# GpSimd takes the first product of three norms and the gated MLP's product, ScalarE the scale and shift

## The chip, the cores and the metric

The kernel runs on one core of a Trainium2 chip. The metric is the device time of one execution in microseconds (us). The kernel before took 2484.61 us, the median of three runs (2483.22 to 2488.88). Five engines work side by side, each in the order of its own queue: TensorE (PE; PEld for its weight loads), VectorE (DVE), ScalarE (ACT), GpSimd (POOL) and SyncE (SP), which issues the large transfers.

## What is computed

A decoder trunk of two layers on 256 tokens of width 2048, all in float32. Every sub-layer is

```python
h = modulate(rms_norm(x, norm_g), shift, scale)   # x / rms * g * (1 + scale) + shift
x = x + gate * sublayer(h)
```

The sub-layers are, in order: a gated MLP (`z = gelu(h @ w_in + b_in)`, `u, v = split(z)`, v goes through a layer norm and a causal mixing over 128 tokens, then `(u * v) @ w_out`), a squared-ReLU MLP, attention with three branches (its keys and values come from a norm of their own, its queries from another), and a second squared-ReLU MLP. A last RMSNorm ends it.

## The kernel before

**Layout.** x lies in SBUF transposed, as 16 tiles `x[:, k, :]` of 128 features by 256 tokens. Every activation that goes into a product is kept as a pair of float32r tiles, `hi` (the rounded value) and `lo` (the rest). Every weight block is split in the same way into `wh` and `wl`, so that each product is three matmuls: wh by hi, wl by hi, wh by lo (L221 to L223).

**The stream.** One queue of 1 MB blocks comes from HBM through the tile `raw`. A weight block is two halves of two k each: ScalarE rounds a half to `wh` (L194), VectorE makes `wl` (L195). Between them lie blocks of the modulation matrices, each one VectorE instruction with an accumulator (L184). `get` keeps up to three halves ready ahead of TensorE. One half feeds 24 matmuls of 256 columns: two k by four output tiles by three.

**The norms.** Where a norm comes ahead of a product there are two ways. In three of the sub-layers (both squared-ReLU MLPs and the key and value projection) the first slab of 512 outputs runs on x scaled without 1/rms (`gemm_first`, L426), and `settle` multiplies 1/rms in afterwards. While that slab runs, from its half 4 on, the normed tiles for the other slabs are made, one closure for each k in `self.todo` (L456), which `norm_until` calls: up to k 5 within the first slab, the other ten in the second slab (`gemm_b`, L226, two k ahead of what TensorE takes). A step of `normed` is three instructions: VectorE multiplies x, 1/rms and the gain (L330), ScalarE adds the shift and rounds to `hi` (L333), VectorE makes `lo` (L334). The intermediate `ht` shares three buffers (tag `t2k`) with the tiles of `settle`, of the rotary embedding and of the MLP. The norm at the start and that of the queries call `normed` directly and are not touched.

**The gated MLP.** In the U half, `mix` (L748) takes a pair of output tiles out of PSUM: two gelu on ScalarE, `u` times the mixed v on VectorE (L755), rounding on ScalarE (L382), low parts on VectorE (L383). There are 16 pairs, in two groups of four slabs, between which the first half of the output product runs. `split` (L380) is the helper that rounds and makes the low parts; it has many other callers.

**Order.** A scheduler arranges the instructions of each engine when the program is built, by program order as priority and its own estimate of when operands are ready; on the chip each queue then runs strictly in that order. So an instruction that waits holds up everything behind it on its engine.

Of the kernel before, what the change touches and what calls it, by code (L numbers as in the profile page):

```python
# [9 lines left out]
F32 = mybir.dt.float32  # L10
F32R = mybir.dt.float32r
AF = mybir.ActivationFunctionType
# [5 lines left out]
T = 256  # L18
KT = D // 128
# [19 lines left out]
def run(gen):  # L39
    for _ in gen:  # L40
        pass
# [21 lines left out]
class Kernel:  # L63
# [259 lines left out]
    def normed(self, rb, g, s, hs, ks=range(KT)):  # L323

        nc = self.nc
        for k in ks:
# [10 lines left out]
            self.last_norm = (hi, lo)  # L337
            hs.append(both)

    def modulation(self, name, g, k0=0, k1=KT):  # L340

        nc = self.nc
        m, b, gs = self.modr[name], self.modb[name], self.modg[name]
        assert all((name, o + k) in self.made for o in (0, KT) for k in range(k0, k1)), name
        for o in (0, KT):
            nc.vector.tensor_add(out=m[:, o + k0:o + k1], in0=m[:, o + k0:o + k1], in1=b[:, o + k0:o + k1])
        nc.vector.scalar_tensor_tensor(
            out=gs[:, k0:k1], in0=m[:, KT + k0:KT + k1], scalar=1.0, in1=g[:, k0:k1], op0=ALU.add, op1=ALU.mult
        )
        return gs, m[:, 0:KT]  # L350
# [26 lines left out]
            for f in range(n * 4 + pair * 2, n * 4 + pair * 2 + 2):  # L377
                nc.scalar.mul(self.x[:, f, :], self.x[:, f, :], self.g_final[:, f:f + 1])

    def split(self, src, hi, lo):  # L380
        nc = self.nc
        nc.scalar.copy(out=hi, in_=src)  # L382
        nc.vector.tensor_sub(out=lo, in0=src, in1=hi.bitcast(F32))  # L383

    def shifted(self, pool, n):

# [39 lines left out]
    def gemm_first(self, hs, evac, spare=False):  # L426

        nc = self.nc  # L430
        if spare:
            row = [self.acc.tile([128, 512], F32, name="acc") for _ in range(2)]
        ps = [self.acc.tile([128, 512], F32, name="acc") for _ in range(4)]
        gs, s, _ = self.coming
        keep = self.keep = self.tmp.tile([128, T], F32, name="rbs", bufs=1)

        def mm(wh, wl, f, k, kk):
            fs = slice(f * 128, (f + 1) * 128)
            (hi, lo), o = self.xs[kk], ps[f]
            nc.tensor.matmul(o[:, 0:T + 2], wh[:, k, fs], hi, start=kk == 0, stop=False, skip_group_check=True)  # L440
            nc.tensor.matmul(o[:, 0:T + 2], wl[:, k, fs], hi, start=False, stop=False, skip_group_check=True)  # L441
            nc.tensor.matmul(o[:, 0:T], wh[:, k, fs], lo, start=False, stop=kk == KT - 1, skip_group_check=True)  # L442

        for half in range(8):
            wh, wl = self.get()
            if half < 7:
                for k in range(2):
                    for f in range(4):
                        mm(wh, wl, f, k, 2 * half + k)
                if half == 3:  # L450
                    if not spare:
                        row = [self.aux.tile([128, 512], F32, name="aux") for _ in range(2)]
                    sd = self.rms_column(row[0])
                elif half == 4:
                    nc.scalar.copy(out=keep, in_=self.rms_row(sd, row[1]))
                    self.todo = iter([lambda k=k: self.normed(keep, gs, s, hs, (k,)) for k in range(KT)])  # L456
                    self.n_normed = 0
                if half >= 4:
                    self.norm_until(2 * half - 6)
            else:  # L460
                for pair in range(2):
                    for f in range(2 * pair, 2 * pair + 2):
                        for k in range(2):
                            mm(wh, wl, f, k, 2 * half + k)
                    evac(pair, ps[2 * pair:2 * pair + 2])
# [153 lines left out]
    def gmlp(self, vec, vp, bv, vctx):  # L619
        tc, nc, A = self.tc, self.nc, self.A  # L620
        b_u, ln_g, ln_b, b_out = vec["b_u"], vec["ln_g"], vec["ln_b"], vec["b_out"]
        with ExitStack() as ctx:
# [7 lines left out]
            hs = []  # L630
# [32 lines left out]
            for at, (slabs, kq) in enumerate(V_ORDER):  # L663
# [5 lines left out]
                keep = at + 1 < len(V_ORDER) and V_ORDER[at + 1][0] is slabs  # L669
# [23 lines left out]
            def layer_norm():  # L693
                for tb in range(2):
                    nc.vector.bn_aggr(out=mv[:, tb, :], in_=stats[:, tb, :, :])
                nc.scalar.activation(out=rs, in_=mv[:, :, 1], func=AF.Sqrt, bias=self.eps)
                nc.vector.reciprocal(out=rs, in_=rs)
                nc.vector.scalar_tensor_tensor(
                    out=mv[:, :, 0], in0=mv[:, :, 0], scalar=-1.0, in1=rs, op0=ALU.mult, op1=ALU.mult
                )  # L700

            def normalise(n):
                for tb in range(2):
                    o = v[:, tb, n * 512:(n + 1) * 512]
                    nc.scalar.activation(
                        out=o, in_=o, func=AF.Identity, scale=rs[:, tb:tb + 1], bias=mv[:, tb, 0:1]
                    )

            def mixed(g):


                w = vs.tile([128, 128], F32, name="ws")
                nc.scalar.dma_start(out=w, in_=A["w_s"][:, g, :])
                nc.gpsimd.affine_select(
                    out=w, in_=w, pattern=[[1, 128]], base=0, channel_multiplier=-1, compare_op=ALU.is_ge, fill=0.0
                )
                bs = vs.tile([128, 128], F32, name="bs")
                src = A["b_s"][g:g + 1, :]
                nc.scalar.dma_start(out=bs, in_=bass.AP(tensor=src.tensor, offset=src.offset, ap=[[0, 128], [1, 128]]))
                rp = self.aux.tile([128, 512], F32, name="aux")  # L720
                nc.tensor.matmul(rp[:, 0:128], self.ones, w, start=True, stop=True)
                mp = self.aux.tile([128, 2, 2, 128], F32, name="aux")
                m = vs.tile([128, 2, 2, 128], F32, name="m")
                for ff in range(2):
                    f = 2 * g + ff
                    for tb in range(2):
                        nc.tensor.matmul(mp[:, ff, tb, :], v[:, tb, f * 128:(f + 1) * 128], w, start=True, stop=True)
                    t = vs.tile([128, 128], F32, name="t", bufs=1)
                    nc.vector.scalar_tensor_tensor(
                        out=t, in0=rp[:, 0:128], scalar=ln_b[:, f:f + 1], in1=bs, op0=ALU.mult, op1=ALU.add  # L730
                    )
                    nc.vector.scalar_tensor_tensor(
                        out=m[:, ff], in0=mp[:, ff], scalar=ln_g[:, f:f + 1],
                        in1=t[:, None, :].to_broadcast([128, 2, 128]), op0=ALU.mult, op1=ALU.add,
                    )
                return m
# [3 lines left out]
            for c in range(2):  # L740
                slabs = []
                for n in range(4 * c, 4 * c + 4):
                    ch = self.slab_tile(n % 4)
                    slabs.append(ch)

                    ms = []

                    def mix(pair, ps, n=n, ch=ch, ms=ms):  # L748
                        u = self.tmp.tile([128, 2, T], F32, name="u", tag="t2k", bufs=3)
                        for ff in range(2):  # L750
                            f = 2 * (n * 2 + pair) + ff
                            nc.scalar.activation(
                                out=u[:, ff, :], in_=ps[:, ff, :], func=AF.Gelu_apprx_tanh, bias=b_u[:, f:f + 1]
                            )
                        nc.vector.tensor_mul(out=u, in0=u, in1=ms[pair].rearrange("p f a b -> p f (a b)"))  # L755
                        self.split(u, ch[pair][:, :, 0, :], ch[pair][:, :, 1, :])

                    for i, _ in enumerate(self.gemm_b(hs, 4, mix)):
                        if i == 4 and n == 0:
                            layer_norm()  # L760
                        if i == 6:
                            normalise(n)
                        if i in (9, 11):
                            ms.append(mixed(n * 2 + len(ms)))
                if gate is None:
                    gate = self.gate("mod_00")
                    nc.vector.tensor_mul(out=gb, in0=gate, in1=b_out)
                    for k in range(KT):
                        nc.scalar.activation(
                            out=self.x[:, k, :], in_=self.x[:, k, :], func=AF.Identity, bias=gb[:, k:k + 1]  # L770
                        )
                run(self.chunk_out(slabs, gate, c == 1, ("mod_01", vec["g_01"])))
# [417 lines left out]
```

## Time and profile before

| | us |
|---|---|
| median of three runs | 2484.61 |
| the profiled execution, whole | 2484.63 |
| its span, first to last instruction | 2482.9 |
| PE busy in the span | 2425.0 |
| VectorE busy | 1860.3 |
| ScalarE busy | 1206.0 |
| GpSimd busy | 57.0 |

The profile describes one execution. Busy times are unions of the instructions' spans on an engine; a wait is put down to the semaphore that came last. The granted clock of TensorE is told as a share of 2.4 GHz, so 0.5 is 1.2 GHz.

### The profile page before, as it was taken

Reading aid. Unit: us, or ns where it says so; the run is one execution under the profiler, and the core shown is the slowest. Engines: PE = TensorE matmul, PEld = TensorE weight load, DVE = VectorE, ACT = ScalarE, POOL = GpSimd, SP = SyncE. Lnnn points to the kernel's source line nnn. Section 1 sums busy time; section 2 is a strip of 40 time slices with the busy share of each in tenths; the row PEclk is TensorE's granted clock in tenths of the full one; section 3 lists DMA queues with packets and bytes.
Section 4 is the critical chain, followed back from the end, with each engine's and each line's share of the span. In section 5 each row is a group of like instructions: output and inputs, shape, how many; then the busy total and the mean of one; then the engine's idle time right before and its main releaser. Section 6 shows DMA issues by size and latency. Waiting matters only on the chain.

```text
span 2482.9 us, 46066 instructions
## 1 busy us (share of the span) xinstructions
PE 2425.0 (98%) x19598; PEld 2337.9 (94%) x19598; DVE 1860.3 (75%) x2330; ACT 1206.0 (49%) x1616; POOL 57.0 (2%) x85
## 2 busy tenths in 40 slices
PE   5999999999999999999999999999999999999998
PEld 3788999999999999999999989889999999999998
DVE  7799988997888878888887679777895455555455
ACT  3445653445543544544555345655653453443553
POOL 0000100020000000000200000000000000000000
PEclk9999999999999999999999999999999999999999
DMA  9895989998798999897985887556695555555352
GB/s 397 318 363 199 347 317 374 338 327 293 288 383 337 349 340 348 334 350 276 348 313 171 304 298 290 193 179 235 235 357 204 189 197 192 190 200 188 127 197 102
DMA packets 99720, 681.82 MB, mean 275 GB/s; under 512 B 11317, under 2 KB 16309, under 8 KB 17593
## 3 DMA queue, kind: packets, MB, share of 16 engines
q1 hardware_dynamic: 92890, 673.25, 73.6%
q10 hardware_dynamic: 6624, 5.63, 0.8%
q8 instruction: 153, 2.51, 0.4%
q14 instruction: 53, 0.43, 0.0%
HBM read 676.74 MB, written 2.10 MB: 273 GB/s over the span
## 4 chain that ended last, share of the span: by engine, by line
PE 87%; DVE 7%; ACT 2%; DMA 2%; issue 2%; DVEq 0%; SPq 0%; ACTq 0%
PE acc L223 24%; PE acc L222 24%; PE acc L221 24%; DVE wl L195 2%; PE acc L252 2%; PE acc L253 2%; PE acc L251 2%; DVE raw L184 2%; PE aux L847 1%; DMA raw<-in_a_w_in 1%; PE acc L440 1%; PE acc L442 1%; PE acc L441 1%; ACT wh L194 1%; PE aux L1050 1%
## 5 line engine op out<-in xcount | busy, mean ns | idle before, releaser
L195 DVE TENSOR_TENSOR wl<-raw,wh 128x1024 fp32r<-128x1024 f32 x816 | 992.4, 1222 | 508.9 <-ACT wh L194 508.3
L194 ACT CAST wh<-raw 128x1024 fp32r<-128x1024 f32 x816 | 854.0, 1051 | 1034.6 <-PE acc L223 797.9
L221 PE MATMUL acc<-hs,wh 128*128 128x256 f32 x3008 | 841.5, 280 | 4.9 <-ACT hs L333 3.6
L223 PE MATMUL acc<-hs,wh 128*128 128x256 f32 x3008 | 834.2, 278 | 7.6 <-DVE hs L334 7.4
L222 PE MATMUL acc<-hs,wl 128*128 128x256 f32 x3008 | 836.9, 279 | 2.2 <-DVE wl L195 2.2
L222 PE MATMUL acc<-ch,wl 128*128 128x256 f32 x2560 | 707.9, 277 | 0.0
L223 PE MATMUL acc<-ch,wh 128*128 128x256 f32 x2560 | 707.8, 277 | 0.0
L221 PE MATMUL acc<-ch,wh 128*128 128x256 f32 x2560 | 707.5, 276 | 0.0
L221 PEld LDWEIGHTS acc<-hs,wh 128*128 128x128 f32 x3008 | 567.7, 189 | 9.7 <-ACT hs L333 4.0
L223 PEld LDWEIGHTS acc<-hs,wh 128*128 128x128 f32 x3008 | 566.8, 189 | 8.8 <-DVE hs L334 8.6
L222 PEld LDWEIGHTS acc<-hs,wl 128*128 128x128 f32 x3008 | 567.7, 189 | 6.3 <-DVE wl L195 3.7
L184 DVE SCALAR_TENSOR_TENSOR raw<-raw,cond 128x2048 f32<-128x2048 f32 x224 | 511.1, 2284 | 5.1 <-DMA raw<-in_mod 4.8
L221 PEld LDWEIGHTS acc<-ch,wh 128*128 128x128 f32 x2560 | 480.9, 188 | 0.0
L223 PEld LDWEIGHTS acc<-ch,wh 128*128 128x128 f32 x2560 | 480.7, 188 | 0.0
L222 PEld LDWEIGHTS acc<-ch,wl 128*128 128x128 f32 x2560 | 480.4, 188 | 0.0
L251 PE MATMUL acc<-wh,hs 128*128 128x512 f32 x256 | 100.7, 398 | 16.1 <-ACT hs L333 16.1
L252 PE MATMUL acc<-wl,hs 128*128 128x512 f32 x256 | 102.6, 401 | 1.1 <-DVE wl L195 0.9
L253 PE MATMUL acc<-wh,hs 128*128 128x512 f32 x256 | 102.1, 400 | 0.0
L364 DVE SCALAR_TENSOR_TENSOR x<-acc,rmod,x 128x256 f32<-128x256 f32 x192 | 80.3, 475 | 10.9 <-PE acc L223 10.9
L251 PEld LDWEIGHTS acc<-wh,hs 128*128 128x128 f32 x256 | 49.0, 192 | 30.7 <-ACT hs L333 17.7
L252 PEld LDWEIGHTS acc<-wl,hs 128*128 128x128 f32 x256 | 49.0, 192 | 13.3 <-DVE wl L195 2.4
L253 PEld LDWEIGHTS acc<-wh,hs 128*128 128x128 f32 x256 | 49.1, 192 | 10.1
(225 smaller groups left out, 1762.2 us busy)
## 6 DMA issues: line engine op xcount, KB each, us to landing
raw<-in_w SPq DMA_DIRECT2D x256, 1024.0 KB, 5.3
raw<-in_mod SPq DMA_DIRECT2D x192, 1024.0 KB, 7.0
raw<-in_a_w_in SPq DMA_DIRECT2D x64, 1024.0 KB, 7.0
raw<-in_a_w_out SPq DMA_DIRECT2D x32, 1024.0 KB, 6.9
raw<-in_mod_kv SPq DMA_DIRECT2D x32, 1024.0 KB, 6.5
raw<-in_w_kv SPq DMA_DIRECT2D x24, 1024.0 KB, 5.1
raw<-in_w_q SPq DMA_DIRECT2D x16, 1024.0 KB, 5.4
raw<-in_w_o SPq DMA_DIRECT2D x16, 1024.0 KB, 5.5
```

The source lines that it names most:

```text
L184: nc.vector.scalar_tensor_tensor(out=raw, in0=raw, scalar=1.0, in1=self.cond, op0=ALU.mult, op1=ALU.mult, accum_out=self.modr[name][:, j:j ...
L194: nc.scalar.copy(out=wh.rearrange("p k n -> p (k n)"), in_=src)
L195: self.splits.append(nc.vector.tensor_sub(out=wl.rearrange("p k n -> p (k n)"), in0=src, in1=wh.rearrange("p k n -> p (k n)").bitcast(F32) ...
L221: nc.tensor.matmul(o, wh[:, k, fs], h[:, 0, :], start=first, stop=False, skip_group_check=True)
L222: nc.tensor.matmul(o, wl[:, k, fs], h[:, 0, :], start=False, stop=False, skip_group_check=True)
L223: nc.tensor.matmul(o, wh[:, k, fs], h[:, 1, :], start=False, stop=last, skip_group_check=True)
L251: nc.tensor.matmul(ps[tb], hi, wh[:, k], start=start and k == 0, stop=False)
L252: nc.tensor.matmul(ps[tb], hi, wl[:, k], start=False, stop=False)
L253: nc.tensor.matmul(ps[tb], lo, wh[:, k], start=False, stop=stop and k == 1)
L364: nc.vector.scalar_tensor_tensor(out=self.x[:, f, :], in0=ps[:, i, :], scalar=gate[:, f:f + 1], in1=self.x[:, f, :], op0=ALU.mult, op1=ALU ...
L440: nc.tensor.matmul(o[:, 0:T + 2], wh[:, k, fs], hi, start=kk == 0, stop=False, skip_group_check=True)
L441: nc.tensor.matmul(o[:, 0:T + 2], wl[:, k, fs], hi, start=False, stop=False, skip_group_check=True)
```

## The change

A new method makes a step of the three norms in four instructions: GpSimd multiplies 1/rms and x, ScalarE scales and shifts in place, ScalarE rounds, VectorE subtracts. In the gated MLP the product u times v and the subtraction that makes its low parts move from VectorE to GpSimd.

```diff
+    def normed_by_pool(self, rb, g, s, hs, k):
+
+        nc = self.nc
+        both = self.hs_tile(self.slots[k])[:, 0:2 * T].rearrange("p (a t) -> p a t", a=2)
+        t = self.tmp.tile([128, T], F32, name="ht", tag="t2k", bufs=3)
+        nc.gpsimd.tensor_mul(out=t, in0=rb, in1=self.x[:, k, :])
+        nc.scalar.activation(out=t, in_=t, func=AF.Identity, scale=g[:, k:k + 1], bias=s[:, k:k + 1])
+        self.split(t, both[:, 0, :], both[:, 1, :])
+        hs.append(both)
+
@@
-    def split(self, src, hi, lo):
+    def split(self, src, hi, lo, eng=None):
         nc = self.nc
         nc.scalar.copy(out=hi, in_=src)
-        nc.vector.tensor_sub(out=lo, in0=src, in1=hi.bitcast(F32))
+        (eng or nc.vector).tensor_sub(out=lo, in0=src, in1=hi.bitcast(F32))
@@
-                    self.todo = iter([lambda k=k: self.normed(keep, gs, s, hs, (k,)) for k in range(KT)])
+                    self.todo = iter([lambda k=k: self.normed_by_pool(keep, gs, s, hs, k) for k in range(KT)])
@@
-                        nc.vector.tensor_mul(out=u, in0=u, in1=ms[pair].rearrange("p f a b -> p f (a b)"))
-                        self.split(u, ch[pair][:, :, 0, :], ch[pair][:, :, 1, :])
+                        nc.gpsimd.tensor_mul(out=u, in0=u, in1=ms[pair].rearrange("p f a b -> p f (a b)"))
+                        self.split(u, ch[pair][:, :, 0, :], ch[pair][:, :, 1, :], nc.gpsimd)
```

## Rows read from the trace of the kernel before

**Rows 1.** Page: the span, and busy time of each engine.
```profile
span 2482.9 us, 46066 instructions
PE 2425.0 (98%) x19598; PEld 2337.9 (94%) x19598; DVE 1860.3 (75%) x2330; ACT 1206.0 (49%) x1616; POOL 57.0 (2%) x85
```

**Rows 2.** Windows: stretch and length; PE, PEld, DVE, ACT, POOL busy; clock; DMA share; GB/s.
```profile
260.00:330.00 70.00, 68.07 (x580) 67.22 (x579) 64.36 (x78) 36.94 (x52) 9.05 (x6) 1.00 0.95 343
440.00:530.00 90.00, 88.98 (x765) 88.21 (x764) 83.67 (x104) 40.07 (x52) 18.61 (x23) 1.00 0.90 327
637.00:663.00 26.00, 23.05 (x190) 22.07 (x189) 24.32 (x39) 16.36 (x29) 0.00 (x0) 1.00 0.66 226
660.00:1310.00 650.00, 650.00 (x5713) 650.00 (x5713) 538.12 (x547) 309.01 (x350) 13.96 (x16) 1.00 0.89 336
1344.00:1368.00 24.00, 18.90 (x142) 18.51 (x142) 22.11 (x40) 13.18 (x21) 0.00 (x0) 0.86 0.40 135
1786.00:1813.00 27.00, 22.62 (x169) 22.02 (x168) 26.67 (x43) 16.28 (x27) 0.00 (x0) 0.87 0.79 278
1798.00:1802.00 4.00, 4.00 (x21) 4.00 (x21) 4.00 (x8) 1.46 (x2) 0.00 (x0) 0.51 0.78 287
```

**Rows 3.** Waits of PE: line, whom for; total us, times, longest us.
```profile
PE acc L223 <- DVE hs L334: 7.4, 4, 4.5
```

**Rows 4.** PE timeline: start, us, instruction, [idle before, releaser].
```profile
1356.15 0.58 PE L223 MATMUL acc<-hs,wh 128*128 128x256 f32 x1 [4.51 <-DVE hs L334]
...
1794.39 0.38 PE L221 MATMUL acc<-hs,wh 128*128 128x256 f32 x1 [3.01 <-ACT hs L333]
```

**Rows 5.** VectorE and ScalarE timelines of the second slab behind two of the norms.
```profile
1351.92 3.78 DVE L835 TENSOR_TENSOR kpk<-kc,pos_k 128x240 f32<-128x240 f32 x8
...
1796.09 0.87 DVE L330 SCALAR_TENSOR_TENSOR ht<-rbs,gmod,x 128x256 f32<-128x256 f32 x2
...
1803.74 0.87 DVE L330 SCALAR_TENSOR_TENSOR ht<-rbs,gmod,x 128x256 f32<-128x256 f32 x2
...
1810.61 0.86 DVE L334 SCALAR_TENSOR_TENSOR hs<-ht,rmod,hs 128x256 fp32r<-128x256 f32 x2
1813.36 0.60 ACT L607 ACTIVATE r<-acc 128x512 f32<-128x512 f32 x1 [1.57 <-PE acc L223]
```

**Rows 6.** Lines by form: count, busy us, mean ns; idle before, releaser.
```profile
L330 DVE SCALAR_TENSOR_TENSOR ht<-rbs,gmod,x 128x256 f32<-128x256 f32 x64 | 28.1, 477 | 0.1
L290 DVE TENSOR_TENSOR ssq<-ssq,sq 128x256 f32<-128x256 f32 x31 | 13.0, 421 | 9.0 <-ACT sq L286 8.2
L755 DVE TENSOR_TENSOR u<-u,m 128x512 f32<-128x512 f32 x16 | 10.7, 695 | 0.6 <-ACT u L752 0.6
L184 DVE SCALAR_TENSOR_TENSOR raw<-raw,cond 128x2048 f32<-128x2048 f32 x224 | 511.1, 2284 | 5.1 <-DMA raw<-in_mod 4.8
L333 ACT ACTIVATE hs<-ht,rmod 128x256 fp32r<-128x256 f32 x64 | 29.2, 502 | 39.5 <-DVE ht L330 39.2
L705 ACT ACTIVATE v<-v,mv,rs 128x512 f32<-128x512 f32 x16 | 12.1, 807 | 1.5 <-DVE mv L698 0.9 <-issue 0.6
L608 ACT ACTIVATE r<-r 128x512 f32<-128x512 f32 x60 | 37.9, 632 | 1.0
L373 ACT ACTIVATE sq<-x 128x256 f32<-128x256 f32 x8 | 2.8, 401 | 0.0
```

**Rows 7.** Lines by form, GpSimd: an instruction by itself, and one among VectorE's work.
```profile
L423 POOL CAST hs<-sh 128x2 fp32r<-128x2 f32 x48 | 35.0, 746 | 776.7 <-PE acc L223 753.1 <-ACT p L1021 21.4 <-DVE wl L195 2.2
masks.py:199 POOL TENSOR_SCALAR_AFFINE_SELECT ident<-ident 128x128 f32<-128x128 f32 x1 | 0.3, 292 | 0.1
```

**Rows 8.** GpSimd and VectorE timelines: a GpSimd instruction that starts with a VectorE one.
```profile
259.35 2.44 POOL L714 TENSOR_SCALAR_AFFINE_SELECT ws<-ws 128x128 f32<-128x128 f32 x1 [17.65 <-DMA ws<-in_w_s]
259.35 2.28 DVE L184 SCALAR_TENSOR_TENSOR raw<-raw,cond 128x2048 f32<-128x2048 f32 x1
```

**Rows 9.** Single lines: count, shortest, median and longest ns, first and last start.
```profile
L383 DVE TENSOR_TENSOR ch<-u,ch x16: 677/684/796, 264.3 to 528.0; 128x512 fp32r<-128x512 f32 x16
L423 POOL CAST hs<-sh x48: 178/593/2332, 503.6 to 1758.2; 128x2 fp32r<-128x2 f32 x48
```

## The prediction

> **What bounds the kernel now.** I read the page first: PE is busy for 2425.0 of 2482.9 us [rows 1]. So the change can only win where PE stands still or runs at a low clock, and 58 us of standing still is all there is; the stretches that the change touches hold 15 us of it, as the next windows show. VectorE, which the change relieves, is busy 75% of the time; that average says nothing about the places where it is the limit. Next I read the windows around the three norms and the two U stretches of the gated MLP [rows 2], then PE's waits [rows 3, 4], then VectorE's queue in order of time [rows 5].
>
> The reader is to see this in the windows. From 660 to 1310 us PE makes 5713 matmuls in 650 us, so 0.114 us each, and the 48 matmuls of one weight block (two halves, four k) take 5.5 us. In the second slab behind each norm it does not reach that: idle 2.95 us at 637 to 663, 5.1 at 1344 to 1368, 4.4 at 1786 to 1813. VectorE is busy for 24.3 of 26, 22.1 of 24 and 26.7 of 27 us there. In the last two the clock also falls after the long stop (4.51 and 3.01 us [rows 4]) to 1.2 GHz, as at 1798 to 1802 (0.51); a mean clock of 0.86 over 24 us and of 0.87 over 27 us costs 3.4 and 3.5 us more. What the norms lose is thus 2.95, 8.5 and 7.9 us, 19 us in all.
>
> VectorE's queue shows why. In the last norm four steps, two L195 and one L184 come round every 7.65 us (from 1796.09 to 1803.74 [rows 5]) against PE's 5.5. The last low parts (k 14 and 15) are ready at 1811.5, and the slab's outputs leave PSUM at 1813.36 [rows 5]: the slab ends when VectorE is through, whatever single wait stands in front. In the first of the three norms the same holds. In the second it is one place: L334 of k 6 stands behind the eight L835 (3.78 us from 1351.92), which are earlier in the program, and PE waits for it [rows 4, 5].
>
> In the U stretches VectorE is busy 64.4 of 70 us and 83.7 of 90, and PE loses 1.9 and 1.0 us [rows 2].
>
> **Part one: a norm step.** Taken from VectorE: L330. Two of them back to back take 0.87 us and one alone 0.477, so one costs 0.39 in the queue [rows 5, 6]. L334 becomes a plain subtraction, 0.421 instead of about 0.477 us (L290, L330 [rows 6]): 0.055 less. Together 0.45 us a step. Added to ScalarE: L333 (0.502) is replaced by an activation with two per-partition operands and a rounding. The nearest row to the first is L705, 0.807 for 512 columns, less 0.231 (L608 less L373) for half the columns: 0.58. The second is near L373, 0.40. So ScalarE gets 0.58 + 0.40 - 0.50 = 0.48 us more a step [rows 6], 7.7 us a norm. It is busy 16.4 of 26 and 16.3 of 27 us in the second slabs [rows 2], and ten of the sixteen steps there add 4.8 us, so it does not become the bound as a whole; it does where `settle` fills it without a gap just ahead of k 6.
>
> Added to GpSimd: a product of two SBUF tiles of 128x256. No row shows one. What rows do show is that GpSimd and VectorE hinder each other. A rounding of 2 columns takes 0.178 us at best, a median of 0.593 and up to 2.33 [rows 9], 0.746 on average [rows 7]. An L714 that starts together with an L184 lasts 2.44 us, to just behind that instruction's end (2.28), and its like by itself takes 0.292 [rows 7, 8]. So a GpSimd instruction that reads SBUF waits until VectorE's instruction with two SBUF operands is over. And the reverse: of the sixteen L383 in the U stretches, which follow upon such an L714 now and then, the longest takes 0.796 us against a median of 0.684 [rows 9]. That is 0.11 us for 128 columns read, 0.88 ns a column. Two operands of 256 columns at that rate hold VectorE for 0.45 us. Ends: below, one operand's time, 0.22, if both are read at once; and nothing at all where VectorE has an operand in PSUM or is idle; above, the fixed 0.18 of the smallest instruction and the reading, 0.63. I take 0.45, since the row that it rests on is the same pair of engines.
>
> So VectorE loses 0.45 us of work a step and is held for 0.45: **the exchange is even**, and the slabs that end with VectorE end when they did. Over the ten steps of a second slab the ends are -2.3 us (0.22) and +1.8 (0.63).
>
> The Trainium skill (SBUF — State Buffer, section Who interferes with whom) says that a VectorE instruction with two SBUF inputs contends with a GpSimd instruction that reads SBUF, and that whoever comes first has the shared ports for the whole instruction. The trace agrees on the waiting, but the L383 that was held up lost 0.11 us while the GpSimd instruction alone takes 0.292, so not the whole instruction. By the page's words a step would hold VectorE for its full length. The Trainium skill (GPSIMD Engine Reference, section 3.1) measures 4497 ns for a two-input add of 2048 columns; an estimate from it is about 0.56 us for 256 columns and 1.1 for 512, and by it the sum below would be some 8 us higher. No run here shows either.
>
> Order: the product leaves VectorE's queue, so it no longer stands behind L184 or L835 there; but `lo` still does, and it now waits for a rounding that waits for an activation that waits for GpSimd. Behind a waiting rounding ScalarE holds the `wh` of the next halves, behind a waiting subtraction VectorE holds `wl`; three halves of lead (8 us) cover that. DMA issues are not passed by anything that moves: SP's queue stays as it is, and GpSimd issues none.
>
> Per norm. First: VectorE even, and k 6 and 7 get 0.9 us later on ScalarE behind `settle`: +0.9 (ends 0 and +2). Second: L334 of k 6 sees one L330 less (-0.4), and the products of k 7 and 8, for which two buffers come free by then, hold the L835 block for 2 x 0.45: +0.5 (ends -4, if the subtraction slips in front of the block, and +2). Third: even, 0 (ends -4, if k 6 is ready early and the clock does not fall, and +3).
>
> **Part two: u times v.** From VectorE: 16 products and 16 subtractions, each about 0.61 us in the queue (0.695 alone, less the 0.085 by which neighbours overlap [rows 5, 6]): -19.5 us. Held by GpSimd: 32 instructions of two operands of 512 columns, 0.90 us each at the rate above: +28.8 (ends 14.4 and, with the fixed part, 34.6). VectorE is not always there to be held (idle 8% and 7% of these stretches, and L729, L732 read PSUM), so I count four fifths, 23: net +3.5 us, ends -8 and +8. VectorE has 5.6 and 6.3 us of idle time in these stretches [rows 2]; about half of an excess falls into it. I take **+2 us** (ends -1 and +5). The chain itself grows by two waits of up to one VectorE instruction each (2.28 us at most [rows 6]), 4 us or so; its reader, the output product, comes to the last slab's tiles after 12 of 16 k, 144 matmuls or 16 us later, so that is covered. Without the cover it would be 4 us once in each of the two groups.
>
> **Sum**: 0.9 + 0.5 + 0 + 2 = 3.4 us on 2484.63, whose profiled execution is within 0.02 us of the median of the runs. About 2488. Ends by the unknowns alone: -9 and +12.
>
> **The rivals.**
> *Norms come free.* GpSimd's reads cost VectorE little (the lower end, 0.22 or less), and k 6 and 7 are ready before PE comes to them, because their products do not queue on VectorE. For it: GpSimd is idle there, and PE's 3.01 us in the third norm are a wait for ScalarE's `hi`, which waits for L330 [rows 4, 6]. [...] With 2.5, 3.5 and 6 us won it gives 2473. Against it: the held L383 and the waits of the 2-column roundings.
>
> *Three buffers and four engines.* A step now holds its `ht` buffer from GpSimd's start to VectorE's subtraction: a wait of 0.6 to 2.2 us behind VectorE, 0.6, 0.58 and 0.40 us, 0.42 us, and up to one `wh` and one `wl` in the queues. That is 3 to 6.5 us, over three buffers 1.0 to 2.2 us a step. PE takes one k in 1.37 us, VectorE lets one through in 1.9 today. From 1.9 on the buffers decide, and VectorE idles in front of its subtraction. At 2.2 the ten steps cost 3 us more a norm, 9 in all, and the first norm's stop is long enough for the clock to fall, 4 us: with part two +15, 2500.
>
> *GpSimd holds the ports for its whole instruction.* Upper ends of both parts: 3 x 1.8 + 0.9 + 0.5 for the norms, and 34.6 x 0.8 - 19.5 = 8 us in the U stretches, of which PE feels about 5: +12, 2496. This is the rule that the Trainium skill (SBUF — State Buffer, section Who interferes with whom) gives. For it: the waits; against it: 0.11 us of holding for an instruction of 0.292.
>
> *The change does nothing*, the first three effects cancelling, is inside the forecast.
>
> **How the numbers follow.** Forecast 0.45 (its own range 2482 to 2492), norms free 0.20, buffers 0.15, whole instruction 0.15, something else 0.05. A measurement of this kernel can tell about 0.2%, 5 us, from no change. The forecast is within that in 0.35 of its 0.45 and slower in 0.10. The first rival is faster (0.19) or just not; the other two are slower (0.30, less 0.02). The rest is spread evenly. Faster 0.21, same 0.40, slower 0.39. Range: 2474 to 2500 leaves out about half of the first rival and a third of the second, 0.1 and 0.06, and the odd ones.
>
> **What would show it.** GpSimd's products of 128x256: length by itself 0.5 to 0.65 us, more where an L195 or L184 runs, and these instructions longer than 1.22 and 2.28 us by 0.2 to 0.6. VectorE still without gaps in the second slabs; ScalarE above 20 us of 27. PE's stops at k 6 of the second norm of the same length. If VectorE shows gaps ahead of L383 of `ht`, the buffers decide; if PE's stops there are gone and the clock stays at 1.0, the norms came free. The prediction is wrong if VectorE's instructions keep their length beside GpSimd's.

## The result, and the profile after

The changed kernel takes 2525.12 us, the median of four runs (2521.31 to 2546.97), where the kernel before, in runs beside it, takes 2486.28: a ratio of 1.0152, with a 95% interval of 1.0109 to 1.0195. That is **39 us slower**; the prediction said 2488 and at most 2500. The profiled execution took 2523.88 us. In some executions, before and after alike, TensorE takes about 3.6% longer for a matmul over some 600 us in which it waits for nothing, some 24 us in all; each difference below is one between executions without that, and a single figure in brackets behind a difference, as in 4.1 (8.2), is the same between executions with it. The interval beside a difference is a 95% bootstrap of the two medians.

The page of the changed kernel (the span; busy time of each engine):

```profile
span 2522.2 us, 46101 instructions
PE 2442.4 (97%) x19598; PEld 2355.2 (93%) x19598; DVE 1845.5 (73%) x2250; ACT 1223.3 (49%) x1664; POOL 162.8 (6%) x165
```

VectorE has 14.8 us less to do than before, including all that GpSimd holds it up [rows 1], and the kernel is 39 us longer. So a lack of VectorE time cannot be the main cause.

Where the time goes is read from the moments at which tiles leave PSUM in both traces. At the last pair of the first group of U slabs the changed kernel is 17.6 us behind (its first Gelu at 355.1 us instead of 337.5), 3 to 5 us for each slab; at the last pair of the second group 32.8 (557.3 for 524.5); the three norms together add 6 to 8. Windows of the changed kernel, at the U stretches and at the three norms, which come 32 to 38 us later than in the kernel before (stretch and length; PE, PEld, DVE, ACT, POOL busy; clock; DMA share; GB/s):

```profile
260.00:330.00 70.00, 63.80 (x519) 63.16 (x518) 49.91 (x55) 31.27 (x43) 23.86 (x17) 0.95 0.84 300
440.00:530.00 90.00, 85.16 (x694) 84.15 (x693) 70.23 (x79) 33.54 (x44) 17.93 (x16) 0.96 0.84 309
669.00:695.00 26.00, 22.09 (x163) 21.48 (x162) 23.69 (x30) 20.84 (x38) 14.45 (x10) 0.87 0.62 222
1380.50:1404.50 24.00, 16.51 (x120) 16.11 (x120) 20.23 (x30) 15.59 (x28) 12.87 (x9) 0.79 0.39 132
1824.00:1851.00 27.00, 19.36 (x144) 18.58 (x142) 26.83 (x34) 20.59 (x37) 14.45 (x10) 0.87 0.69 252
```

Beside [rows 2] the reader sees three things in the first line. TensorE makes 519 matmuls where it made 580. VectorE is busy 49.9 us of 70, where it was busy 64.4: it is idle. And the transfers, which ran at a share of 0.95, run at 0.84: the stream itself has been held up. In the two U windows TensorE stands still for 8 us more than before, and its lower clock (0.95 and 0.96 for 1.00) costs another 7. In the norms TensorE's clock is lower than before in the first two (0.87 and 0.79 for 1.00 and 0.86), and it stops more often; ScalarE is busy for 20.8 and 20.6 us, as forecast.

The waits that answer to [rows 3] (line, whom for; total us, times, longest us), TensorE's first, then ScalarE's and GpSimd's:

```profile
PE aux L737 <- DVE m L742: 16.9, 6, 3.4
...
PE acc L223 <- DVE hs L393: 12.8, 6, 4.8
PE acc L221 <- ACT hs L392: 7.0, 3, 3.2
...
ACT ch L392 <- POOL u L765: 33.1, 16, 4.0
...
ACT ht L346 <- POOL ht L345: 24.8, 17, 5.9
...
POOL ht L345 <- DVE hs L393: 18.1, 21, 3.6
```

The first line is where TensorE loses most in the gated MLP: its mixing product waits for VectorE's `m`. The same line of the kernel before:

```profile
PE aux L727 <- DVE m L732: 1.3, 4, 0.5
```

The fourth line is the one that matters most for the cause: all 16 roundings of the gated MLP wait on ScalarE for GpSimd's product, 33.1 us in all. Before, three of them waited for VectorE's product, 1.7 us in all. Behind them VectorE waits for `wh`; its waits from 255 to 345 us, before and after:

```profile
DVE wl L195 <- ACT wh L194: 5.0, 6, 1.7
DVE wl L195 <- ACT wh L194: 20.6, 10, 4.3
```

What a wait of this kind does, in the second U slab: ScalarE's timeline, then GpSimd's, VectorE's, SP's and one line of TensorE's (start, us, instruction, [idle before, releaser]):

```profile
288.79 0.84 ACT L762 ACTIVATE u<-acc,vecs 128x256 f32<-128x256 f32 x2 [0.74 <-DMA raw<-in_a_w_in]
290.21 0.47 ACT L762 ACTIVATE u<-acc,vecs 128x256 f32<-128x256 f32 x1 [0.57 <-PE acc L223]
293.09 0.62 ACT L392 CAST ch<-u 128x512 fp32r<-128x512 f32 x1 [2.41 <-POOL u L765]
293.62 0.47 ACT L762 ACTIVATE u<-acc,vecs 128x256 f32<-128x256 f32 x1
293.99 1.04 ACT L194 CAST wh<-raw 128x1024 fp32r<-128x1024 f32 x1
298.71 0.62 ACT L392 CAST ch<-u 128x512 fp32r<-128x512 f32 x1 [3.68 <-POOL u L765]
299.23 3.89 ACT L194 CAST wh<-raw 128x1024 fp32r<-128x1024 f32 x4
310.02 1.04 ACT L194 CAST wh<-raw 128x1024 fp32r<-128x1024 f32 x1 [6.89 <-DMA raw<-in_a_w_in]
```

```profile
289.72 3.34 POOL L765 TENSOR_TENSOR u<-u,m 128x512 f32<-128x512 f32 x1 [2.16 <-ACT u L762]
294.81 0.29 POOL L724 TENSOR_SCALAR_AFFINE_SELECT ws<-ws 128x128 f32<-128x128 f32 x1 [1.75 <-DMA ws<-in_w_s]
295.08 2.36 POOL L393 TENSOR_TENSOR ch<-u,ch 128x512 fp32r<-128x512 f32 x1
297.39 1.28 POOL L765 TENSOR_TENSOR u<-u,m 128x512 f32<-128x512 f32 x1
```

```profile
289.62 2.28 DVE L184 SCALAR_TENSOR_TENSOR raw<-raw,cond 128x2048 f32<-128x2048 f32 x1
...
295.06 1.23 DVE L195 TENSOR_TENSOR wl<-raw,wh 128x1024 fp32r<-128x1024 f32 x1 [3.14 <-ACT wh L194]
300.32 1.47 DVE L195 TENSOR_TENSOR wl<-raw,wh 128x1024 fp32r<-128x1024 f32 x1 [4.04 <-ACT wh L194]
...
303.92 2.35 DVE L195 TENSOR_TENSOR wl<-raw,wh 128x1024 fp32r<-128x1024 f32 x2
...
308.40 1.22 DVE L195 TENSOR_TENSOR wl<-raw,wh 128x1024 fp32r<-128x1024 f32 x1
...
310.02 0.48 DVE L742 SCALAR_TENSOR_TENSOR m<-aux,vecs,t 128x256 f32<-128x256 f32 x1
```

```profile
291.94 0.33 SPq L157 DMA_DIRECT2D raw<-in_a_w_in  x1
296.31 0.33 SPq L157 DMA_DIRECT2D raw<-in_mod  x1
304.02 0.33 SPq L157 DMA_DIRECT2D raw<-in_a_w_in  x1
```

```profile
310.56 1.18 PE L737 MATMUL aux<-ws,v 128*128 128x128 f32 x4 [3.45 <-DVE m L742]
```

Read them from the top. The first rounding (293.09) waits for a product of 3.34 us, which starts with an L184 (289.62) and ends 1.2 us behind it; alone it takes 1.28. The second stands behind more: GpSimd's queue holds a masking of the next slab's w_s (L724), which waits for its transfer until 294.81, and then a low part, before the second product begins. Behind the two roundings wait five wh copies (293.99 and the four at 299.23). So VectorE waits for wh, 3.14 and 4.04 us; the raw tiles come free late; SP issues nothing from 296.31 to 304.02; and up to 310.02 ScalarE itself waits 6.89 us for a block. As far as weights go, the three halves of lead carry TensorE over the pause, if barely: it takes the `wl` that is ready at 301.79 from 301.84 on. But `m` (310.02) stands in VectorE's queue behind the `wl` of halves that TensorE takes only later: those that start at 305.06 (the second of the two at 303.92) and 308.40 it takes from 314.56 and 317.38 on. So at 310.56 TensorE has stood still for 3.45 us, waiting for `m`, with two halves of weights ready. In the U stretches its waits for weights come to 0.9 us, those for `m` to 16.9. The lead covers the weights and not `m`.

GpSimd's lines by form in the changed kernel (count | busy us, mean ns | idle before):

```profile
L345 POOL TENSOR_TENSOR ht<-rbs,x 128x256 f32<-128x256 f32 x48 | 60.4, 1272 | 170.4 <-ACT rbs L465 129.0 <-DVE hs L393 18.1 <-DVE ch L393 11.4
...
L765 POOL TENSOR_TENSOR u<-u,m 128x512 f32<-128x512 f32 x16 | 29.8, 1864 | 30.3 <-ACT u L762 30.3
L393 POOL TENSOR_TENSOR ch<-u,ch 128x512 fp32r<-128x512 f32 x16 | 22.8, 1428 | 8.8 <-ACT ch L392 8.8
```

The shortest L345 takes 0.73 us, the shortest L765 1.28; the rest of the means is read as waiting for VectorE. And VectorE is held: two L195 that take 2.35 us (303.92 above) took 3.71, and an L184 that takes 2.28 [rows 8] took 3.39, each beside GpSimd instructions of 128x512:

```profile
265.97 3.71 DVE L195 TENSOR_TENSOR wl<-raw,wh 128x1024 fp32r<-128x1024 f32 x2 [2.38 <-ACT wh L194]
269.60 3.39 DVE L184 SCALAR_TENSOR_TENSOR raw<-raw,cond 128x2048 f32<-128x2048 f32 x1
```

### The profile page after: what moved, and what is told of

It is laid out like the page before. It is cut to its first block, busy times and chain, and to the rows that moved or that the text cites. A ratio compares the mean times of both kernels' runs of the same rounds, so it can differ in the third digit from the quotient of the medians.

```text
span 2522.2 us, 46101 instructions
## 1 busy us (share of the span) xinstructions
PE 2442.4 (97%) x19598; PEld 2355.2 (93%) x19598; DVE 1845.5 (73%) x2250; ACT 1223.3 (49%) x1664; POOL 162.8 (6%) x165
## 4 chain that ended last, share of the span: by engine, by line
PE 79%; DVE 8%; issue 7%; ACT 3%; DMA 2%; POOL 2%; DVEq 0%; SPq 0%; ACTq 0%; POOLq 0%
PE acc L222 22%; PE acc L223 22%; PE acc L221 22%; DVE wl L195 3%; DVE raw L184 2%; PE acc L252 2%; PE acc L251 2%; PE acc L253 2%; PE aux L857 1%; ACT wh L194 1%; DMA raw<-in_a_w_in 1%; DMA ws<-in_w_s 1%; PE aux L1060 1%; POOL ht L345 1%; PE aux L737 1%
## 5 line engine op out<-in xcount | busy, mean ns | idle before, releaser
L195 DVE TENSOR_TENSOR wl<-raw,wh 128x1024 fp32r<-128x1024 f32 x816 | 1005.3, 1237 | 552.8 <-ACT wh L194 551.7
L223 PE MATMUL acc<-hs,wh 128*128 128x256 f32 x3008 | 841.9, 280 | 12.8 <-DVE hs L393 12.8
L184 DVE SCALAR_TENSOR_TENSOR raw<-raw,cond 128x2048 f32<-128x2048 f32 x224 | 513.9, 2296 | 4.8 <-DMA raw<-in_mod 4.4
L251 PE MATMUL acc<-wh,hs 128*128 128x512 f32 x256 | 101.0, 398 | 16.1 <-ACT hs L333 16.1
L251 PEld LDWEIGHTS acc<-wh,hs 128*128 128x128 f32 x256 | 49.1, 192 | 30.8 <-ACT hs L333 17.7
L433 POOL CAST hs<-sh 128x2 fp32r<-128x2 f32 x48 | 34.2, 729 | 646.3 <-PE acc L223 643.8
L345 POOL TENSOR_TENSOR ht<-rbs,x 128x256 f32<-128x256 f32 x48 | 60.4, 1272 | 170.4 <-ACT rbs L465 129.0
```

What stands on the lines that cost most here:

```text
L184: nc.vector.scalar_tensor_tensor(out=raw, in0=raw, scalar=1.0, in1=self.cond, op0=ALU.mult, op1=ALU.mult, accum_out=self.modr[name][:, j:j ...
L195: self.splits.append(nc.vector.tensor_sub(out=wl.rearrange("p k n -> p (k n)"), in0=src, in1=wh.rearrange("p k n -> p (k n)").bitcast(F32) ...
L223: nc.tensor.matmul(o, wh[:, k, fs], h[:, 1, :], start=False, stop=last, skip_group_check=True)
L251: nc.tensor.matmul(ps[tb], hi, wh[:, k], start=start and k == 0, stop=False)
L345: nc.gpsimd.tensor_mul(out=t, in0=rb, in1=self.x[:, k, :])
L433: nc.gpsimd.tensor_copy(out=t[:, T:T + 2], in_=sh[:, k, :])
```

## The experiments

**Theory 1**: ScalarE's queue is held in order behind roundings that wait for GpSimd, and the stream behind it is late. **Rival**: GpSimd's reads hold VectorE, which is near its limit in these stretches. For the norms: ScalarE's added work, the three buffers, or the holding.

All runs together (difference of the medians to before, us; ScalarE's waits for u at the roundings; VectorE's busy time less that of before; the last two columns are read from one profiled execution each):

| kernel | difference | interval | ScalarE's waits | VectorE busy |
|---|---|---|---|---|
| the change | +37.6 | +33 to +42 | 33.1 | -14.8 |
| the change, again | +37.6 | +33 to +41 | 36.3 | -15.6 |
| norms only | +9.5 | +6 to +13 | 2.4 | -5.7 |
| gated MLP only | +27.6 | +24 to +31 | 35.5 | -9.7 |
| roundings later by program | +22.6 | +21 to +30 | 30.7 | -7.5 |
| roundings in the next slab by program | +18.8 | +16 to +23 | 25.6 | -5.8 |
| product only on GpSimd | +18.9 | +17 to +21 | 25.7 | -6.7 |
| masking behind the low parts | +17.3 | +13 to +22 | 26.2 | -4.6 |
| rounding on GpSimd too | +15.8 | +12 to +19 | 0 | +12.8 |
| 16 spare products | +8.4 | +5 to +12 | 1.8 | +16.1 |
| low parts only on GpSimd | +4.2 | +2 to +8 | 3.7 | +2.9 |
| no waits in the gated MLP | +4.1 | -1 to +11 | 0 | +8.5 |
| norms, product on VectorE | -2.5 | -6 to +4 | 1.6 | -2.5 |
| norms, two steps a buffer | +1.8 | -2 to +8 | 1.7 | -3.3 |
| the change, all three repaired | +12.6 | +8 to +16 | 0 | +2.8 |
| before, additions behind | -8.0 | -12 to -5 | 1.7 | +0.4 |

**One part alone.** The norms' line goes back to `normed` (gated MLP only), or the two lines of `mix` go back to VectorE (norms only).

> Only the norms are changed; the gated MLP is as before. The lag of the changed kernel's PSUM evacuations behind those of before grows by some 31 us in the two U stretches and by 6 to 8 us behind the norms. If the two parts are independent: 2491 to 2494 us. If the norms suffer only because the stream of weights reaches them late out of the gated MLP: 2484 to 2488.

> Only the gated MLP's product and low parts are on GpSimd; the norms are as before. If the parts are independent: 2514 to 2519 us, nearly all of the loss. If the norms' part is larger than the lag shows: below 2508.

Ratios of 1.0038 (1.0023 to 1.0052) and 1.0110 (1.0094 to 1.0126). The parts add up: 9.5 + 27.6 = 37.1 of 37.6 us; the norms' 2497.1 us are 3 us above what the lag had led to expect. The gated MLP is three quarters of the loss.

**What holding VectorE costs.** One spare product of GpSimd for each pair, over a tile that nothing reads any more:

```diff
+nc.gpsimd.tensor_mul(out=ms[pair]..., in0=ch[pair][:, :, 0, :], in1=ch[pair][:, :, 1, :])
```

> The kernel before, with one more GpSimd product of two 128x512 SBUF tiles (high part times low part, written over m, which nothing reads any more) behind each of the 16 pairs; nobody waits for it. It prices the holding of VectorE alone: 16 times 1.1 us, with nothing taken from VectorE, about what the change adds to VectorE net (32 x 1.1 x 0.8 - 19.5 = +9) and more. Theory 1: the stretches have some slack, +2 to +9 us, 2487 to 2494. Rival (holding VectorE is what costs): +20 to +30, 2505 to 2515.

Measured: +8.4 us, a ratio of 1.0035 (1.0022 to 1.0048). Its page, and the wait of TensorE that grew:

```profile
PE 2425.4 (97%) x19598; PEld 2337.9 (94%) x19598; DVE 1876.4 (75%) x2330; ACT 1205.0 (48%) x1616; POOL 89.0 (4%) x101
```

```profile
PE aux L727 <- DVE m L732: 10.3, 7, 2.0
```

VectorE is busy for 16.1 us more, so each product of 128x512 holds it for 1.0 us, and half of that is felt. The place is the mixing product, which waits for the `m` that VectorE makes: 1.3 us in the kernel before, 10.3 here. So the holding is real, with a price of about half a us for each in this order. The change itself has VectorE busy for less, not more, so this price does not give its 27.6 us.

**Later roundings.** The rounding is put off in the program: behind the second pair and the next slab's second block, then (second run, `i in (5, 7)`) behind its third and fourth.

```diff
-self.split(u, ch[pair]..., nc.gpsimd)
+due.append(lambda: self.split(u, ch[pair]..., nc.gpsimd))
...
+if due and i in (3, 15):
+    due.pop(0)()
```

> As the kernel with the gated MLP's part alone, but the rounding of u times m stands later in ScalarE's program: that of the first pair behind the second pair's Gelus, that of the second pair behind the first two blocks of the next slab. GpSimd does the same work, and VectorE is held as often. Theory 1 (ScalarE is held up in order behind a rounding that waits for GpSimd, 2.4 to 5.9 us at a time, so wh, raw buffers and the stream of weights are late): most of the loss goes, 2486 to 2496 us. Rival (VectorE is held by GpSimd's reads, some 1.1 us for each of 32 instructions): nothing is won, 2512 to 2520.

> As the kernel with the gated MLP's part alone, but both roundings of a slab stand in ScalarE's program behind the third and fourth block of the next slab (8 us later). Putting them one to two blocks later won 5 of 27.6 us, but there ScalarE still waited 15.1 us for GpSimd in one U stretch, since GpSimd makes two products in a row. Here ScalarE should not wait at all. Theory 1 (ScalarE held in order): 2489 to 2498 us, of which some 4 us are the holding of VectorE that the spare products priced. Rival (the holding of VectorE, or GpSimd's length): 2508 to 2516 as with the smaller delay.

Measured +22.6 and +18.8, which looks like the rival. The traces say that neither did what it was meant to: ScalarE still waited 30.7 and 25.6 us. In the built order the scheduler had moved the roundings forward again, to behind one wh copy or even in between the Gelus; why is not shown. Neither run tells the theories apart; what they show is that the loss shrank with the wait.

**Half of the work.** The product alone on GpSimd, or the low parts alone.

> Only the product on GpSimd, the low parts on VectorE: the rounding on ScalarE waits for GpSimd as in the change, the holding is halved. Theory 1: most of the loss stays, 2505 to 2515 us. Rival (holding): about half, 2499 to 2503.

> Only the low parts of u times m on GpSimd; the product stays on VectorE, so that nothing on ScalarE waits for GpSimd. VectorE is held 16 times 1.1 us and relieved of 16 times 0.6. Theory 1: 2486 to 2493 us. Rival (holding): about half of the loss, 2499 to 2503.

GpSimd does 16 instructions of the same size in both. With the product there, ScalarE waits 25.7 us and the loss is 18.9. With the low parts there, for which ScalarE has nothing to wait, VectorE is busier by 9.6 us than in the other, and the loss is 4.2. The rival wanted both near half; theory 1 wanted this difference. The product's 2504.3 us lie between the two ranges, a us from either; it is the low parts' 2489.6 that tell them apart. With the product alone the low parts on VectorE wait too, 39.7 us for all roundings of `ch` (18.5 before), so ScalarE's queue is not the only one that a waiting instruction holds there.

**No rounding on ScalarE.** `nc.gpsimd.tensor_copy` makes the high part.

> The gated MLP's part alone, with the rounding of u times m on GpSimd too, so that ScalarE never waits for GpSimd there; GpSimd gets 16 copies of 128x512 more. Theory 1: 2490 to 2500 us, in spite of more work on GpSimd. Rival (holding of VectorE): above 2516, by 16 more instructions that read SBUF.

Measured +15.8, 2501, a us above theory 1's range and far from the rival's. ScalarE no longer waits there, and VectorE's waits for `wh` are as before (5.3 us from 255 to 345, 5.0 before). Yet VectorE is busy for 12.8 us more than before, and the mixing products wait for `m` for 14.3 us, where they waited 1.3. So these 15.8 us are not theory 1's wait. By the price of the spare products the holding would be 6 to 7 of them; the other 9 stay open. It may matter which of VectorE's instructions are held, those ahead of `m` or others; no run here separates that.

**No waits at all.** `issue_after` ties each rounding to the third or fourth wh copy behind the Gelus, which the scheduler can't undo, and the masking to the low parts ahead of it. The other run ties the masking alone.

```diff
+with tc.issue_after(self.last_wh):
+    due.pop(0)()
...
+with tc.issue_after(self.last_low):
     nc.gpsimd.affine_select(out=w, in_=w, ...)
```

> The gated MLP's part alone; each of its roundings is put behind the third or fourth wh copy after the Gelus on ScalarE's queue, which the earlier attempt to delay them did not reach (there the scheduler let only one wh copy pass), and GpSimd's masking of w_s, which waits for a DMA, is put behind the low parts, so that it no longer stands between the two products. GpSimd does all its work, ScalarE has nothing to wait for. Two causes would explain all runs so far: holding VectorE costs 0.48 us per us of net holding (8.4 us for 16 spare products of 1.1 us), so (35.2 - 19.5) x 0.48 = 7.5 us, and ScalarE's waits cost the other 20. Then this gives 2491 to 2499 us. Rival (length of the chain through GpSimd, or a higher price of the holding): 2505 or more.

> The gated MLP's part alone, roundings where the change has them; only the masking of w_s on GpSimd is put behind the low parts. In the changed kernel it stood between or ahead of the products in 5 of 8 slabs and waited 1.8 to 2.7 us for its DMA there, which delayed a rounding by some 11 us in all. If these waits count in full: 2502 to 2508 us. If what counts is GpSimd's wait for VectorE (3.3 us for a product that starts with a 2.28 us VectorE instruction): 2511 to 2516, as without it.

With both, 27.6 us become 4.1 (8.2), within what was expected of the two causes. No rounding waits for GpSimd, and these lines show what is left: the page, and TensorE's waits at the mixing:

```profile
PE 2453.1 (97%) x19598; PEld 2365.5 (94%) x19598; DVE 1868.8 (74%) x2298; ACT 1204.8 (48%) x1616; POOL 124.3 (5%) x117
```

```profile
PE aux L734 <- POOL ws L727: 4.4, 3, 2.8
PE aux L740 <- DVE m L745: 3.9, 5, 1.1
```

GpSimd does all the work of the gated MLP's part in 124.3 us, more than the 107.1 that it was busy for with that part as the change has it, and VectorE is held for longer; only the order has changed. That **settles the greater part of the gated MLP**: the order costs 19 to 24 us. The 4 to 8 that are left are not all holding: of TensorE's waits, 3.9 us are for `m`, and 4.4 are for the `w_s` whose masking this very run has put later. The masking alone is worth 10 us of the order (27.6 to 17.3): a GpSimd instruction that waits for a 64 KB transfer stood ahead of a product in GpSimd's queue.

**The norms.** The product by 1/rms on VectorE again, in the new form of four instructions; and two steps sharing one of the three buffers, so that six can be under way. The gated MLP is as before in both.

```diff
-nc.gpsimd.tensor_mul(out=t, in0=rb, in1=self.x[:, k, :])
+nc.vector.tensor_mul(out=t, in0=rb, in1=self.x[:, k, :])
```

```diff
+if k % 2 == 0:
+    self.two = self.tmp.tile([128, 2, T], F32, name="ht", tag="t2k", bufs=3)
+t = self.two[:, k % 2]
```

> Only the norms are changed, in the new form of four instructions, but with the product by 1/rms on VectorE. ScalarE has its added 0.48 us a step as in the change; nothing waits for GpSimd, nothing is held. If the norms' 9.5 us come from ScalarE's added work: 2493 to 2499. If from GpSimd (its waits and the holding): 2485 to 2490.

> Only the norms are changed, product on GpSimd, but two steps share one of the three buffers, so that six steps can be under way instead of three. If the buffers decide (in the changed kernel GpSimd waits some 20 us for VectorE's subtraction to free one, in each of two norms): most of the 9.5 us goes, 2486 to 2490. If the chain of four instructions or ScalarE's work decides: 2494 to 2500.

ScalarE's added work costs nothing that shows: it is busy 1225.4 us where it was 1206.0, and the time is 2.5 us less (-6 to +4); with the product on VectorE the three buffers are enough. With six steps under way 9.5 us become 1.8 (4.4), 2491 us, a us above its range. GpSimd's waits for a buffer and ScalarE's for the product, which were 18.1 and 24.8 us over the three norms, are then:

```profile
POOL ht L347 <- DVE hs L395: 10.1, 6, 3.0
...
ACT ht L348 <- POOL ht L347: 15.5, 10, 6.2
```

**All three repaired**, in the whole change, and the change beside it on the same chip.

> The whole change, all products and low parts on GpSimd as it has them, with three edits of order and buffers alone: the gated MLP's roundings behind the third or fourth wh copy, the masking of w_s behind the low parts, two norm steps a buffer. If the causes found one by one are all there is: the holding in the gated MLP (4 to 8 us) and the norms' rest (2 to 4 us) remain, 6 to 12 us above before. Rival (something in the whole change that the parts do not show): 20 us or more above before.

> The changed kernel as it is, on the same chip as its repaired form: 36 to 40 us above before.

+12.6 (10.9) against +37.6 (36.5), just above the 6 to 12 that were expected. Three edits of order and buffers, with every instruction of the change still there, take back 25 us. What remains is about the sum of the two remainders, 4 to 8 and 2 to 4. How it divides is open; TensorE's waits there are, besides those for `m`, for the later masking and for the norms' low parts (7.4 us in the kernel before [rows 3]):

```profile
PE acc L223 <- DVE hs L395: 11.8, 7, 4.9
...
PE aux L736 <- POOL ws L729: 4.7, 3, 2.7
PE aux L742 <- DVE m L747: 4.0, 5, 1.4
```

**A kernel that beats both.** The prediction had put the second norm's stop down to one place [rows 4, 5]. In the kernel before, the eight additions are tied, in pairs, behind low parts:

```diff
+                    yield
...
-blocks("k", kc)
-run(self.gemm_b(hs, 4, ...))
+steps = blocks("k", kc)
+for i, _ in enumerate(self.gemm_b(hs, 4, ...)):
+    if i in (4, 6, 8, 10):
+        with tc.issue_after(self.last_norm[1]):
+            next(steps)
+            next(steps)
```

> The kernel before, with the eight additions L835 of the second norm's slab (3.78 us in one block on VectorE, ahead of the low parts of k 6) put in pairs behind the low parts of k 7, 9, 11 and 13. If that block is what TensorE waits for at 1356.15 us (4.51 us, and the clock at half speed behind it, 3.4 us more): 4 to 8 us below before. If VectorE's total work in that slab decides: within 2 us of before.

2479.59 us, 8.0 below before. The window 1336 to 1366 of the kernel before and of this one:

```profile
1336.00:1366.00 30.00, 24.90 (x192) 24.51 (x191) 28.11 (x55) 18.58 (x30) 0.00 (x0) 0.89 0.36 122
```

```profile
1336.00:1366.00 30.00, 28.29 (x237) 27.54 (x237) 29.62 (x55) 19.15 (x32) 0.00 (x0) 1.00 0.46 159
```

TensorE makes 237 matmuls instead of 192 and its clock stays at 2.4 GHz, with VectorE making the same 55 instructions. For this stop, where that work stands decides, and not how much of it there is.

## Why the prediction was wrong, point by point

- **Part two, the chain.** This is the step that failed. It read: "The chain itself grows by two waits [...], 4 us or so; its reader, the output product, comes [...] 16 us later, so that is covered." No wait of the output product for its tiles shows. But the waiting instruction is a rounding on ScalarE, and behind it stand the wh copies of the whole stream. The step asked who reads the result, and not what is queued behind the one who waits, and so put this at nothing. The prediction had named that very queue for the norms, and let "three halves of lead (8 us) cover that". The lead does cover the weights: TensorE waits 0.9 us for them in the U stretches. It does not cover `m`, which stands in VectorE's queue behind weights that TensorE takes later, and there TensorE waits 16.9 us; its clock falls besides (0.95 and 0.96). Measured: 33.1 us of waits on ScalarE, 19 to 24 us of time, the masking's 10 (next point) among them.
- **GpSimd's own queue.** Of transfers the prediction said only that SP's queue stays as it is "and GpSimd issues none". GpSimd issues no transfers, but its maskings wait for some, and [rows 8] shows one for which GpSimd had been idle 17.65 us until the transfer came. A product behind such an instruction is as late as the transfer. This was not in the sum at all; it is worth 10 us.
- **Part two, the holding.** The account was 19.5 us less work and 23 of holding, +3.5 net. Without the waits VectorE is busy 8.5 us more, so the holding is 28: 0.88 an instruction, where 0.90 had been worked out, and the discount to four fifths was wrong. That about half of it is felt was right in the spare products (8.4 of 16.1 us); by that the term is about 4 us instead of 2, inside its ends. With the rounding on GpSimd too, 15.8 us were lost at 12.8 of it, which the half does not give. In the change as it stands the holding is smaller, because VectorE is idle, waiting for ScalarE.
- **GpSimd's instructions.** "0.5 to 0.65 us" alone for 128x256 measured 0.73. An estimate from the Trainium skill (GPSIMD Engine Reference, section 3.1), 0.56 and 1.1 us, falls short of 0.73 and 1.28 by nearly the same, 0.16 or 0.17, close to the 0.178 of the smallest GpSimd instruction [rows 9]. On who holds whom, the page's rule (the Trainium skill, SBUF — State Buffer, section Who interferes with whom) is nearer than the prediction was: the L184 at 269.60 lost 1.1 us to a GpSimd instruction that takes 1.3 by itself, not a part like the 0.11 of 0.292. That made the rival "whole instruction" right in its mechanism, and 12 us still far from 39.
- **Part one, the exchange.** Right: with the norms alone VectorE is busy 5.7 us less over 48 steps, 0.12 a step, about even. ScalarE's work grows by 0.40 us a step (19.4 over 48), 0.48 said, and it does not become the bound, as said.
- **Part one, the sum.** +1.4 was forecast, +9.5 came. The rival "three buffers and four engines", given 0.15, is what the runs bear out: with room for six steps most of it goes. It had priced the norms at 13 us, 9 for the buffers and 4 for the clock. The sign to watch for was badly chosen: "VectorE shows gaps ahead of L383 of `ht`". The waits stand at GpSimd, 18.1 us for a buffer, and at ScalarE; VectorE's queue has other work to fill its gaps.
- **The first rival, norms come free.** It counted 12 us as won, part of that by a clock that stays up. No run shows that: in the changed kernel the mean clock at the three norms is 0.87, 0.79 and 0.87.
- **The second norm.** The stop stayed, as said, and its place was right, as the last run shows.
- **The falsifier.** "The prediction is wrong if VectorE's instructions keep their length beside GpSimd's": they did not, and the prediction was wrong all the same. It tested the one mechanism that had been priced.

## What to carry to other kernels

Before moving an operation to another engine, list what is queued behind every instruction that will wait for it, on the waiting engine and on the new one; the readers of its result are only half of the question. A lead of some blocks covers the reader of those blocks; a reader of something else that stands in the same queue behind them, like `m` here, has no cover, so look where it stands. And when an edit is meant to move an instruction, read the built order in the trace before reading its time.

## What was not expected of the hardware

GpSimd with two operands in SBUF and VectorE hold each other up both ways and in large pieces. A GpSimd product of 128x512 takes 1.28 us alone and 3.34 when it starts with an L184; sixteen spare products made VectorE busy for 16.1 us more, 1.0 us for each. Moving 32 instructions that cost VectorE some 0.61 us apiece to GpSimd left VectorE 8.5 us busier once nothing else was in the way. No arrangement here in which GpSimd took this work was measurably faster than VectorE doing it.
